# A 31-tap convolution on VectorE: three half-length filters with taps placed by hand, in a two-layer encoder

## The chip, the core and the metric

The kernel runs on one core of one Trainium2 chip. The metric is the device time of one execution in microseconds: 2544.08 us, the median of 3 runs (2543.35 to 2545.97). The engines are named as in the profile: PE (TensorE, matrix products), PEld (its weight loads), DVE (VectorE), ACT (ScalarE), POOL (GpSimd), SP (SyncE, which issues most DMAs).

## The reference

Input x is 1 x 1024 x 1024 (tokens by width) in float32; there are two layers. Each has a mixing part of three head groups, fed by one projection, and a feed-forward part.

```
for l in range(2):
    z = rms_norm(x, norm_mix[l]) @ w_in[l]        # 1024 -> 2560, 20 tiles of 128 columns
    (q_a, k_a, v_a, q_h, i_h, f_fw, f_bw, g_h, a_c, g_c) = split(z)
    o_att = attention(rope(rms_norm(q_a)), rope(rms_norm(k_a)), v_a)   # 8 heads, 2 for keys
    o_hg  = hgrn2_bidirectional(q_h, i_h, f_fw, f_bw, g_h)             # gated recurrence, both ways
    o_cv  = conformer_conv(a_c, g_c)
    x = x + concat[o_att, o_hg, o_cv] @ w_out[l]
    x = x + square(relu(rms_norm(x) @ w1[l])) @ w2[l]

def conformer_conv(a, gate, w_dw, b_dw, ln_g, ln_b):
    u = a * sigmoid(gate)                 # 256 channels x 1024 tokens
    y = depthwise convolution of u with w_dw, 31 taps, padded by 15 on both sides
    y = layer_norm(y + b_dw, ln_g, ln_b)  # over the channels
    return silu(y)
```

With taps w[-15] to w[15], the convolution of one channel is y[t] = sum over d of w[d] u[t + d], tokens outside 0 to 1023 being zero.

## The kernel before

Activations lie with channels on the 128 partitions and the 1024 tokens along the row, so a projection tile is 128 x 1024 float32: two banks of PSUM. A layer starts with 20 such tiles (`ztile`, `zsteps`), each 48 matmuls of 128x512 (L223: 8 slices of the input, three passes with high and low parts, two halves). DVE evacuates a tile by multiplying it with the norm's factors (L322, `evac`); two buffers of PSUM (S) serve the tiles in turn, so PE can be one tile ahead of DVE. For each tile DVE also makes the low part of the next weights (L200, wlo).

The order of a layer's first part in the program: tiles 16 and 18, 17 and 19 (`conv_in(0)`, `conv_in(1)`: two blocks of 128 channels), each pair giving u = a * sigmoid(s), by ACT and by POOL (L337). Then `Hgrn(0)`, half of the recurrence, takes tiles 6, 10, 12, 14, 8: from them come X (four arrays of 1024 tokens), T (decays), hks, the gate and iv, and iv is transposed on PE (L442) in the constructor. `core()` then runs it: `near()` (neighbouring tokens, L453 to L473), seven levels s = 1, 2, 4 to 64 of a doubling scheme, each with two multiplications of X on POOL and two on DVE (L525) and one of T (L526), and from s = 2 on with copies on ACT (L482), scores on PE (L494) and a masked write of them (L501, L505, predicated copies). Behind the levels stand Tc (L531, a copy of the decays), the transposes of the keys (L539), the chain of states (L555, L558) and the output (L583 on PE, L587 on DVE). Between these steps the loop at L702 asks two generators in turn, twice each: `qg`, the attention's projections (tile 5 for values, 4 for keys, 0 to 3 for queries, with statistics in `rstd`, L151 to L156, a rotation L621 to L624 and, for keys, L660), and `cg`, the convolution.

`conv(i)` is 31 DVE instructions on a row of 1024 for one block of channels: a first tap at d = 0 (L344, with the bias), then 30 taps (L352), each adding a shifted u times one weight to y in place:

```
nc.vector.scalar_tensor_tensor(
    y[:, lo:hi], u[:, lo + d : hi + d], par[:, l, wof + tap : wof + tap + 1], y[:, lo:hi],
    op0=ALU.mult, op1=ALU.add,
)
yield
```

After both blocks `conv_tail` takes the layer norm: token sums on PE (L162 in `tok_sums`), `rstd`, a widening copy on ACT (L168 in `widen`), a turn by PE (L178 in `flip`), and the subtraction or multiplication on DVE; the second half of it does the same for the squares.

Behind the loop `while not ys[1:]` (L706) finishes the second block. Then come `Hgrn(1)`, the recurrence's other half, with tiles 7, 11, 13, 15, 9 (its core is spread over the attention stage), the first two score units of the attention (`att_scores`) between its tiles 15 and 9, and the attention itself: 64 units. The projection w_out and the feed-forward part follow; the change touches nothing there.

The program's order is not the engines' order. The scheduler of the tile framework places each instruction on its engine by its place in the program and by its own estimates of when its inputs are there, so a tap that is asked for late in the program may come to stand earlier on DVE, between instructions that would wait. Buffers come from pools (x8: 8 rows of 128 x 1024, tmp: 4; small tiles nwa and nwt: 2 each), and a tile whose buffer is still in use waits for it.

## Time and profile before

| | |
|---|---|
| median of 3 runs | 2544.08 us (2543.35 to 2545.97) |
| profiled execution, its own time | 2543.87 us |
| its span, first to last instruction | 2541.9 us |
| PE busy | 2457.1 us (97%) |
| DVE busy | 1995.0 us (78%) |
| ACT busy | 1205.0 us (47%) |
| POOL busy | 736.7 us (29%) |

The profile is one execution seen by the hardware's profiler. Busy time is a sum over the span; an engine's share says little about a single stage, so the rows further down are cut into stages: from 58.66 us (the evacuation of the last tile of `conv_in`) over 117.61 (the evacuation of iv, behind the last tile of `Hgrn(0)`) and 221.17 (the states' chain) to 263.03 (the first evacuation of `Hgrn(1)`), 304.30 and 559.59 (most of the attention). The second layer's same points are 1321.70, 1380.60, 1483.80, 1525.60, 1566.90 and 1819.00. The time of the profiled execution and not the span is what compares with the median.

### The profile page before, as it was taken

To read this page: it belongs to the slowest core of one execution; us is meant where nothing else is said; L and a number is where in the kernel's file an instruction comes from. 1 tells how busy PE (TensorE), PEld (TensorE's weight loads), DVE (VectorE), ACT (ScalarE), POOL (GpSimd) and SP (SyncE) were. 2 spreads that over 40 slices of the span, in tenths; PEclk is the share of its full clock that TensorE was granted. 3 is DMA by queue.
4 is the path that set the end of the run, shared out by engine and by line. 5 is a ranking of instruction groups with operands and counts; after the bars stand their busy time and mean duration, and the time that the engine had idled before them with its cause. 6 is when DMAs were issued, how large, how long until landed. Compare 5 with 4: busy or idle time off the path is not lost.

```text
span 2541.9 us, 34037 instructions
## 1 busy us (share of the span) xinstructions
PE 2457.1 (97%) x12608; PEld 2023.4 (80%) x12608; DVE 1995.0 (78%) x3051; ACT 1205.0 (47%) x1960; POOL 736.7 (29%) x463
## 2 busy tenths in 40 slices
PE   8989989999999999999999899999999999999999
PEld 7777778878788887888887777788787888878887
DVE  5998598872887778987859985898628777789876
ACT  4222478773544444443433224787635444444332
POOL 0232565433034430000123324665330354300000
PEclk9999999999999999999999999999999999999999
DMA  4101210033244448454131113000322544584542
GB/s 149 68 25 63 95 43 18 14 106 115 75 165 164 144 158 322 159 174 156 67 108 50 42 63 104 17 18 26 124 84 91 178 141 154 185 287 158 162 153 91
DMA packets 113078, 286.99 MB, mean 113 GB/s; under 512 B 11409, under 2 KB 11665, under 8 KB 112913
## 3 DMA queue, kind: packets, MB, share of 16 engines
q1 hardware_dynamic: 112912, 284.83, 32.4%
q8 instruction: 99, 1.62, 0.3%
q14 instruction: 67, 0.54, 0.1%
HBM read 197.75 MB, written 87.03 MB: 112 GB/s over the span
## 4 chain that ended last, share of the span: by engine, by line
PE 78%; DVE 15%; ACT 3%; issue 2%; POOL 2%; DMA 0%; SPq 0%; DVEq 0%; ACTq 0%; POOLq 0%
PE S L223 15%; PE S L1196 10%; PE c L995 10%; PE S L995 7%; PE e L995 7%; PE e L1196 6%; PE c L1196 6%; DVE x L352 4%; PE e L803 4%; PE c L782 3%; PE S L745 3%; PE e L494 2%; DVE P L756 1%; PE e L162 1%; PE e L583 1%
## 5 line engine op out<-in xcount | busy, mean ns | idle before, releaser
L223 PE MATMUL S<-xs,whi 128*128 128x512 f32 x1280 | 366.3, 407 | 10.6 <-ACT xs L208 9.1
L223 PEld LDWEIGHTS S<-xs,whi 128*128 128x128 f32 x1280 | 245.0, 195 | 67.5 <-ACT xs L208 9.1
L1196 PE MATMUL S<-xs,xs 128*128 128x512 f32 x816 | 201.6, 390 | 2.6 <-DVE xs L897 2.6
L223 PE MATMUL S<-xs,wlo 128*128 128x512 f32 x640 | 204.0, 399 | 0.0
L896 ACT ACTIVATE xs<-m 128x512 fp32r<-128x512 f32 x216 | 126.0, 619 | 141.6 <-DVE m L907 50.8
L761 POOL TENSOR_SCALAR P<-P,mx 128x1024 f32<-128x1024 f32 x124 | 142.6, 1150 | 164.1 <-DVE mx L760 126.2
L787 DVE TENSOR_TENSOR PT<-c,PT 128x512 fp32r<-128x512 f32 x256 | 171.1, 684 | 24.2 <-ACT PT L786 22.6
L1196 PEld LDWEIGHTS S<-xs,xs 128*128 128x128 f32 x816 | 152.8, 188 | 35.5 <-DVE xs L897 3.5
L786 ACT ACTIVATE PT<-c 128x512 fp32r<-128x512 f32 x256 | 147.5, 593 | 69.1 <-PE c L782 65.5
L199 ACT ACTIVATE whi<-raw 128x1024 fp32r<-128x1024 f32 x56 | 59.1, 1058 | 247.1 <-PE S L223 234.1
L803 PE MATMUL e<-PT,x 128*128 128x256 f32 x1024 | 172.3, 297 | 0.8 <-ACT PT L786 0.5
L756 DVE TENSOR_SCALAR_CACHE_REDUCE P<-S,nqc 128x1024 f32<-128x1024 f32 x124 | 158.5, 1278 | 14.0 <-PE S L745 8.8
L352 DVE SCALAR_TENSOR_TENSOR x<-x,par,x 128x1009 f32<-128x1009 f32 (+14 forms) x120 | 166.8, 1390 | 1.8
L782 PE MATMUL c<-cons,P 128*128 128x128 f32 x992 | 152.4, 278 | 10.5 <-POOL P L761 5.6
L897 DVE TENSOR_TENSOR xs<-m,xs 128x512 fp32r<-128x512 f32 x216 | 144.9, 694 | 22.0 <-ACT xs L896 22.0
L745 PE MATMUL S<-x,QS 128*128 128x512 f32 x480 | 154.0, 419 | 4.8 <-DVE P L756 4.5
L260 POOL TENSOR_TENSOR tmp<-tmp,tmp 128x1024 f32<-128x1024 f32 x19 | 50.6, 2662 | 360.4 <-ACT tmp L259 360.2
L759 ACT ACTIVATE P<-P,mx 128x1024 f32<-128x1024 f32 x124 | 142.4, 1149 | 24.3 <-DVE P L756 23.0
L803 PEld LDWEIGHTS e<-PT,x 128*128 128x128 f32 x1024 | 139.0, 193 | 8.5 <-ACT PT L786 2.0
L223 PEld LDWEIGHTS S<-xs,wlo 128*128 128x128 f32 x640 | 123.2, 193 | 27.1 <-issue 0.3
L782 PEld LDWEIGHTS c<-cons,P 128*128 128x128 f32 x992 | 115.3, 141 | 36.7 <-issue 10.6
L1196 PE MATMUL e<-xs,xs 128*128 128x512 f32 x552 | 140.6, 390 | 0.3 <-DVE xs L897 0.3
(310 smaller groups left out, 5639.1 us busy)
## 6 DMA issues: line engine op xcount, KB each, us to landing
m<-ad SPq DMA_DIRECT2D x104, 512.0 KB, 3.8
ad<-x SPq DMA_DIRECT2D x176, 256.0 KB, 2.2
raw<-w_in_t SPq DMA_DIRECT2D x40, 512.0 KB, 3.4
xs<-w_t SPq DMA_DIRECT2D x36, 512.0 KB, 3.7
raw<-w_t SPq DMA_DIRECT2D x36, 512.0 KB, 3.7
m<-w_t SPq DMA_DIRECT2D x32, 512.0 KB, 6.8
ad<-tmp SPq DMA_DIRECT2D x48, 256.0 KB, 2.2
x<-w_t SPq DMA_DIRECT2D x24, 512.0 KB, 4.6
```

The costliest lines, as they stand in the source:

```text
L223: nc.tensor.matmul(zp[h] if type(zp) is list else zp[:, h, :], w, xx[:, h * 512 : (h + 1) * 512], start=first, stop=last)
L352: nc.vector.scalar_tensor_tensor(y[:, lo:hi], u[:, lo + d : hi + d], par[:, l, wof + tap : wof + tap + 1], y[:, lo:hi], op0=ALU.mult, op1= ...
L745: nc.tensor.matmul(S[:, hb, :], qs, kk[:, hb * 512 : (hb + 1) * 512], start=first, stop=not first)
L756: nc.vector.tensor_scalar(Pt, S, nqc[:, j, ci : ci + 1], 3.0e38, op0=ALU.mult, op1=ALU.min, accum_out=mx[:, 1:2])
L761: nc.gpsimd.tensor_scalar(Pt, Pt, mx[:, 3:4], 0.0, op0=ALU.mult, op1=ALU.add)
L782: nc.tensor.transpose(t[:, q * P : (q + 1) * P], Pt[:, hb, q * P : (q + 1) * P], ident)
L786: nc.scalar.activation(hi, src, AF.Copy)
L787: nc.vector.tensor_tensor(lo, src, hi.bitcast(F32), op=ALU.subtract)
L803: nc.tensor.matmul(pvp[:, cs], VS[g][:, hb * 4 + kb, :], pt[:, kb, :], start=hb == 0 and n == 0, stop=hb == 1 and n == 7,)
L897: ordered("v", nc.vector.tensor_tensor(lo, src, hi.bitcast(F32), op=ALU.subtract))
L995: nc.tensor.matmul(bank, w[i][:, kt * P : (kt + 1) * P], BC[name][kt][j], start=n == 0 and name not in ("M6", "M7", "M3"), stop=n == 11, s ...
L1196: nc.tensor.matmul(banks[dt], w[i][:, dt * P : (dt + 1) * P], a[j], start=n == 0 and name not in ("M6", "M7", "M3"), stop=n == 3 * SG - 1, ...
```

## The change

The convolution is computed in another way, and its instructions get other places.

Another way: the tokens are split into even ones ue and odd ones uo, 512 each. POOL writes u in this order (first all even tokens, then all odd ones). With s[n] = uo[n-1] + ue[n], the even taps as one filter E, the odd taps as one filter O and the sums of neighbouring taps as a third, a block of channels takes three filters of half the length: 15 taps on ue, 16 on uo and 16 on s. The even outputs are E(ue) + O(uo); the odd outputs are the third filter's result less the other two, with a correction at the row's end (`edge`). The third filter is written in place of uo. The bias comes in with the last combination, which writes y with every second token.

Other places: `taps(n)` asks the convolution's generator for n steps (two pieces each) at fixed points of the constructor of `Hgrn(0)` (6, 6, 6, 6, 5) and of `Hgrn(1)` (3, 4, 4, 4); in the loop of the core it is asked once in every second step after the fourth. A piece is also held behind the last instruction on the list `mark` (a level's predicated copy or the multiplication of T) by an order-only dependency. The transposes of iv move from the constructor to `turned()`, called in `near()` after its first step. The statistics of the keys are taken up at step 6 instead of 2 of the next tile, and `while not ys[1:]` is gone.

```diff
-            nc.gpsimd.tensor_tensor(u, a, s, op=ALU.mult)
+            nc.gpsimd.tensor_tensor(
+                u.rearrange("p (h n) -> p n h", h=2), a.rearrange("p (n h) -> p n h", h=2),
+                s.rearrange("p (n h) -> p n h", h=2), op=ALU.mult,
+            )
             us.append(u)
+        mark = []
+        def after_gate(i):
+            if mark:
+                tc.add_manual_dep(i.ins, mark[-1].ins.name, mybir.DependencyInfo(
+                    mybir.DependencyClass.NoSync, mybir.DependencyReason.DATA), reason="order")
+        def fir(dst, src, taps, shift=0):
+            n, m = dst.shape[1], src.shape[1]
+            for k, (d, w) in enumerate(sorted(taps, key=lambda t: abs(t[0] + shift))):
+                d += shift
+                lo, hi = max(0, -d), min(n, m - d)
+                if k == 0:
+                    nc.vector.tensor_scalar(dst, src[:, d : d + n], w, 0.0, op0=ALU.mult, op1=ALU.add)
+                else:
+                    after_gate(nc.vector.scalar_tensor_tensor(
+                        dst[:, lo:hi], src[:, lo + d : hi + d], w, dst[:, lo:hi], op0=ALU.mult, op1=ALU.add
+                    ))
+                yield
+        def conv_steps(i):
+            H = 512
+            ue, uo = halves(us[i])
+            both, mix = x8(), x8()
+            even, odd = halves(both)
...
+            hs = cst.t([P, 16], "nwa", bufs=2)
+            edge = cst.t([P, 16], "nwt", bufs=2)
...
+            s = mix[:, 0 : H + 1]
...
+            nc.vector.tensor_tensor(s[:, 1:H], uo[:, 0 : H - 1], ue[:, 1:H], op=ALU.add)
+            yield
+            second = fir(even, ue, [(d, tap(2 * d)) for d in range(-7, 8)])
+            for _ in fir(odd, uo, [(d, tap(2 * d + 1)) for d in range(-8, 8)]):
+                yield
+                if next(second, 1) is None:
+                    yield
+            yield from fir(uo, s, [(d, hs[:, d + 8 : d + 9]) for d in range(-8, 8)], 1)
+            y = mix.rearrange("p (n h) -> p n h", h=2)
+            cb = pv(l, "cb", i)
+            nc.vector.scalar_tensor_tensor(y[:, :, 0], even, cb, odd, op0=ALU.add, op1=ALU.add)
+            yield
+            nc.vector.tensor_tensor(uo[:, 0 : H - 1], uo[:, 0 : H - 1], even[:, 1:H], op=ALU.subtract)
+            nc.vector.tensor_tensor(uo[:, H - 1 : H], uo[:, H - 1 : H], edge[:, 8:9], op=ALU.subtract)
+            yield
+            nc.vector.scalar_tensor_tensor(y[:, :, 1], uo, cb, odd, op0=ALU.add, op1=ALU.subtract)
+            ys.append(mix)
+            yield
+
         def conv(i):
-            u = us[i]
-            y = x8()
...
+            for k, _ in enumerate(conv_steps(i)):
+                if k % 2:
+                    yield
+        def taps(n):
+            for _ in range(n):
+                next(cg, None)
...
                 evac(ztile(6 + ls), hq)
+                taps(3 if ls else 6)
...
-                    if ls == 1:
-                        next(cg, None)
...
+                    taps(4 if ls else 6)
...
+                if ls == 0:
+                    taps(5)
+
+            def turned(self):
                 for h in range(2):
                     tpv = pse()
...
                 yield
+                self.turned()
...
-                    if k == 2 and rest:
+                    if rest and k == (6 if col == 4 else 2):
...
-        for _ in h0.core():
-            for g in (qg, cg, qg, cg):
-                next(g, None)
+        for n, _ in enumerate(h0.core()):
+            next(qg, None)
+            if n > 3 and n % 2:
+                taps(1)
+            next(qg, None)
         drain(qg)
-        while not ys[1:]:
-            next(cg)
+        mark.clear()
```

What stands on the engines is shown at three places (a row is line, operation, written tile, read tiles, shape, count; lines are those of each kernel's own file).

DVE of the first layer, ahead of the evacuation of iv (the L322 that writes an m tile). Before, whole taps of block 0 stand between the evacuations of tiles 14 (tmp) and 8 (m); x_135 is its y, x_79 its u:

```order
L322 TENSOR_TENSOR tmp_651<-S_116_658,Rb_307 128x1024
L200 TENSOR_TENSOR wlo_717<-raw_714,whi_716 128x1024
L352 SCALAR_TENSOR_TENSOR x_135_807<-x_79_341,par_76,x_135_807 128x1017
L352 SCALAR_TENSOR_TENSOR x_135_807<-x_79_341,par_76,x_135_807 128x1016
L352 SCALAR_TENSOR_TENSOR x_135_807<-x_79_341,par_76,x_135_807 128x1015
L352 SCALAR_TENSOR_TENSOR x_135_807<-x_79_341,par_76,x_135_807 128x1014
L352 SCALAR_TENSOR_TENSOR x_135_807<-x_79_341,par_76,x_135_807 128x1013
L352 SCALAR_TENSOR_TENSOR x_135_807<-x_79_341,par_76,x_135_807 128x1012
L322 TENSOR_TENSOR m_118_713<-S_122_720,Rb_307 128x1024
```

With the change, these rows lead up to the same evacuation of iv; they are the end of block 0's third filter (x_79 is now the odd half that is written over, x_102 the tile of s and y) and its four combinations (L396, L393, L395 and L398 of the new file):

```order
L200 TENSOR_TENSOR wlo_775<-raw_772,whi_774 128x1024
L358 SCALAR_TENSOR_TENSOR x_79_341<-x_102_526,nwa_527,x_79_341 128x508
L358 SCALAR_TENSOR_TENSOR x_79_341<-x_102_526,nwa_527,x_79_341 128x506
L358 SCALAR_TENSOR_TENSOR x_79_341<-x_102_526,nwa_527,x_79_341 128x507
L358 SCALAR_TENSOR_TENSOR x_79_341<-x_102_526,nwa_527,x_79_341 128x505
L358 SCALAR_TENSOR_TENSOR x_79_341<-x_102_526,nwa_527,x_79_341 128x506
L396 TENSOR_TENSOR x_79_341<-x_79_341,nwt_528 128x1
L358 SCALAR_TENSOR_TENSOR x_79_341<-x_102_526,nwa_527,x_79_341 128x505
L393 SCALAR_TENSOR_TENSOR x_102_526<-x_101_525,par_76 128x512
L395 TENSOR_TENSOR x_79_341<-x_79_341,x_101_525 128x511
L398 SCALAR_TENSOR_TENSOR x_102_526<-x_79_341,par_76,x_101_525 128x512
L322 TENSOR_TENSOR m_122_771<-S_126_778,Rb_307 128x1024
```

Six taps of 1012 to 1017 tokens stood there; now pieces of some 506 tokens stand there, and block 0 is finished before iv is evacuated.

DVE behind Tc, in the statistics of the queries (nwa, nwt, nwy: `rstd`). Before, x_200 is block 1's y, m_227 the states:

```order
L154 SCALAR_TENSOR_TENSOR nwt_1563<-nwy_1562 128x16
L558 SCALAR_TENSOR_TENSOR m_227_1493<-m_227_1493,Tc_1490,e_1583 128x64
L155 TENSOR_TENSOR nwt_1563<-nwt_1563,nwa_1561 128x16
L352 SCALAR_TENSOR_TENSOR x_200_1289<-x_91_460,par_76,x_200_1289 128x1018
L156 SCALAR_TENSOR_TENSOR nwy_1562<-nwt_1563,nwy_1562 128x16
L558 SCALAR_TENSOR_TENSOR m_227_1493<-m_227_1493,Tc_1490,e_1583 128x64
L154 SCALAR_TENSOR_TENSOR nwt_1563<-nwy_1562 128x16
L352 SCALAR_TENSOR_TENSOR x_200_1289<-x_91_460,par_76,x_200_1289 128x1017
L155 TENSOR_TENSOR nwt_1563<-nwt_1563,nwa_1561 128x16
L558 SCALAR_TENSOR_TENSOR m_227_1493<-m_227_1493,Tc_1490,e_1583 128x64
L156 SCALAR_TENSOR_TENSOR nwy_1562<-nwt_1563,nwy_1562 128x16
L555 COPY m_227_1493<-e_1621 128x64
```

With the change, behind its Tc, the statistics of a query tile alternate with pieces of block 1's first filters (x_127 holds even and odd, x_91 is u):

```order
L156 SCALAR_TENSOR_TENSOR nwy_1469<-nwt_1470,nwy_1469 128x16
L358 SCALAR_TENSOR_TENSOR x_127_832<-x_91_460,par_76,x_127_832 128x506
L154 SCALAR_TENSOR_TENSOR nwt_1470<-nwy_1469 128x16
L358 SCALAR_TENSOR_TENSOR x_127_832<-x_91_460,par_76,x_127_832 128x506
L155 TENSOR_TENSOR nwt_1470<-nwt_1470,nwa_1468 128x16
L358 SCALAR_TENSOR_TENSOR x_127_832<-x_91_460,par_76,x_127_832 128x506
L156 SCALAR_TENSOR_TENSOR nwy_1469<-nwt_1470,nwy_1469 128x16
L358 SCALAR_TENSOR_TENSOR x_127_832<-x_91_460,par_76,x_127_832 128x505
L154 SCALAR_TENSOR_TENSOR nwt_1470<-nwy_1469 128x16
L358 SCALAR_TENSOR_TENSOR x_127_832<-x_91_460,par_76,x_127_832 128x505
L155 TENSOR_TENSOR nwt_1470<-nwt_1470,nwa_1468 128x16
L358 SCALAR_TENSOR_TENSOR x_127_832<-x_91_460,par_76,x_127_832 128x505
```

Two taps of block 1 stood among twelve rows; now six pieces do, each between two dependent small instructions.

PE of the first layer, at the second turn of `conv_tail` (L162 the token sums of the squares, L178 the turn of the widened factors). Before:

```order
L162 MATMUL e_2026<-cons_77,tmp_1959 128x1 x8
L223 MATMUL S_310_2089<-xs_103,whi_1878 128x512 x2
L223 MATMUL S_310_2089<-xs_104,whi_1878 128x512 x2
L223 MATMUL S_310_2089<-xs_103,wlo_1879 128x512 x2
L223 MATMUL S_310_2089<-xs_115,whi_1878 128x512 x2
L223 MATMUL S_310_2089<-xs_116,whi_1878 128x512 x2
L223 MATMUL S_310_2089<-xs_115,wlo_1879 128x512 x2
L223 MATMUL S_310_2089<-xs_120,whi_1878 128x512 x2
L223 MATMUL S_310_2089<-xs_121,whi_1878 128x512 x2
L223 MATMUL S_310_2089<-xs_120,wlo_1879 128x512 x2
L223 MATMUL S_310_2089<-xs_125,whi_1878 128x512
L178 MATMUL e_2051<-cons_77,tmp_2049 128x128 x4
```

With the change (L802 are the first scores of the attention, S_319 and S_322):

```order
L802 MATMUL S_319_2206<-x_274_1849,x_272_1841 128x512 x2
L162 MATMUL e_2150<-cons_77,tmp_2086 128x1 x8
L802 MATMUL S_319_2206<-x_275_1850,x_272_1841 128x512 x2
L802 MATMUL S_322_2217<-x_274_1849,x_272_1841 128x512 x2
L802 MATMUL S_322_2217<-x_275_1850,x_272_1841 128x512 x2
L178 MATMUL e_2175<-cons_77,tmp_2173 128x128 x4
L178 MATMUL e_2182<-cons_77,tmp_2173 128x128 x4
```

Before, 19 projection matmuls stood between the sums and the turn; now 6 score matmuls do.

## Rows read from the trace of the kernel before

**Rows 1.** The page: busy time of the engines; the chain by engine and line.
```profile
PE 2457.1 (97%) x12608; PEld 2023.4 (80%) x12608; DVE 1995.0 (78%) x3051; ACT 1205.0 (47%) x1960; POOL 736.7 (29%) x463
...
PE 78%; DVE 15%; ACT 3%; issue 2%; POOL 2%; DMA 0%; SPq 0%; DVEq 0%; ACTq 0%; POOLq 0%
PE S L223 15%; PE S L1196 10%; PE c L995 10%; PE S L995 7%; PE e L995 7%; PE e L1196 6%; PE c L1196 6%; DVE x L352 4%; PE e L803 4%; PE c L782 3%; PE S L745 3%; PE e L494 2%; DVE P L756 1%; PE e L162 1%; PE e L583 1%
```

**Rows 2.** Windows by stage: window, length, busy us, clock, DMA.
```profile
core 0: us, PE busy (x) PEld busy (x) DVE busy (x) ACT busy (x) POOL busy (x), PEclk, DMA share, GB/s
58.66:117.61 58.95, 55.95 (x247) 45.98 (x245) 56.87 (x43) 16.48 (x16) 11.37 (x4) 1.00 0.20 72
117.61:221.17 103.56, 91.80 (x519) 72.75 (x519) 99.87 (x136) 29.22 (x43) 40.42 (x19) 0.90 0.13 44
221.17:263.03 41.86, 40.93 (x309) 32.60 (x310) 34.87 (x68) 8.28 (x10) 11.54 (x3) 0.96 0.18 64
...
1380.60:1483.80 103.20, 92.06 (x519) 73.02 (x519) 96.79 (x135) 29.26 (x43) 40.07 (x19) 0.90 0.13 44
...
304.30:559.59 255.29, 243.90 (x1689) 205.58 (x1690) 213.51 (x406) 194.80 (x338) 148.15 (x115) 0.99 0.14 45
1566.90:1819.00 252.10, 240.36 (x1660) 202.06 (x1661) 210.77 (x403) 192.02 (x334) 148.55 (x115) 0.99 0.13 41
```

**Rows 3.** The chain of waits, 60 to 330 us: by line; start, us, what.
```profile
by line: PE S L223 26.9%; DVE x L352 17.7%; issue 8.5%; DVE wlo L200 4.9%; PE e L162 4.5%; DVE X L525 3.8%; DVE A L505 3.4%; DVE tmp L322 2.7%; PE e L583 2.7%; DVE T L526 2.3%; DVE nwt L154 2.0%; DVE nwt L155 1.7%; DVE tmp L623 1.6%; DVE tm
...
58.85 10.67 PE S L223 x47
```

**Rows 4.** Waits, 58.66 to 263.03 us: us in total, times, longest us.
```profile
DVE ms L678 <- PE e L162: 7.0, 4, 2.9
...
PE e L637 <- DVE A L501: 4.2, 1, 4.2
```

**Rows 5.** Lines of DVE, 58.66 to 263.03 us: busy us, mean ns, idle before.
```profile
L352 DVE SCALAR_TENSOR_TENSOR x<-x,par,x 128x1009 f32<-128x1009 f32 (+14 forms) x60 | 83.5, 1392 | 0.9
...
L344 DVE TENSOR_SCALAR x<-x,par 128x1024 f32<-128x1024 f32 x2 | 3.7, 1844 | 0.0
```

**Rows 6.** Timeline of DVE: start us, us, instruction and count.
```profile
71.81 9.14 DVE L352 SCALAR_TENSOR_TENSOR x<-x,par,x 128x1012 f32<-128x1012 f32 x7
...
118.74 1.28 DVE L453 TENSOR_TENSOR m<-X 128x512 f32<-128x512 f32 x2
119.94 2.53 DVE L200 TENSOR_TENSOR wlo<-raw,whi 128x1024 fp32r<-128x1024 f32 x1
...
179.89 0.17 DVE L156 SCALAR_TENSOR_TENSOR nwy<-nwt,nwy 128x16 f32<-128x16 f32 x1
180.01 1.28 DVE L352 SCALAR_TENSOR_TENSOR x<-x,par,x 128x1022 f32<-128x1022 f32 x1
181.21 0.01 DVE L621 LOAD_MASK_SELECT tmp<-tmp  x1
```

**Rows 7.** Lines of DVE, whole span: ns min/median/max; a form, mean ns.
```profile
L344 DVE TENSOR_SCALAR x<-x,par x4: 804/806/2882, 61.4 to 1411.9; 128x1024 f32<-128x1024 f32 x4
...
L1008 DVE SCALAR_TENSOR_TENSOR x<-x,Rb 128x512 f32<-128x512 f32 x64 | 42.5, 684 | 0.1
```

**Rows 8.** DVE and POOL: two timelines, one line, one group.
```profile
98.99 5.93 DVE L352 SCALAR_TENSOR_TENSOR x<-x,par,x 128x1020 f32<-128x1020 f32 x3
...
99.15 3.38 POOL L449 TENSOR_TENSOR m<-m,m 128x1024 f32<-128x1024 f32 x1 [35.41 <-DVE m L423]
...
L337 POOL TENSOR_TENSOR x<-tmp,tmp x4: 2394/2508/2877, 44.2 to 1324.1; 128x1024 f32<-128x1024 f32 x4
...
L525 POOL TENSOR_TENSOR X<-X,T 128x512 f32<-128x512 f32 x14 | 24.5, 1769 | 37.0 <-ACT m L482 25.3 <-DVE m L453 6.8 <-DVE T L526 4.9
```

**Rows 9.** Waits of PE, whole span: us in total, times, longest us.
```profile
PE e L442 <- DVE m L322: 11.4, 4, 4.3
PE e L178 <- ACT tmp L168: 7.9, 4, 2.8
```

More of the change, by code (lines that the diff above doesn't have):

```diff
@@ L336, in conv_in @@
             u = x8()
-            nc.gpsimd.tensor_tensor(u, a, s, op=ALU.mult)
+            nc.gpsimd.tensor_tensor(
+                u.rearrange("p (h n) -> p n h", h=2), a.rearrange("p (n h) -> p n h", h=2),
+                s.rearrange("p (n h) -> p n h", h=2), op=ALU.mult,
+            )
             us.append(u)
-        def conv(i):
-            u = us[i]
-            y = x8()
-            wof = PAR["cw"][0] + i * CK
-            nc.vector.tensor_scalar(
-                y, u, par[:, l, wof + CPAD : wof + CPAD + 1], pv(l, "cb", i), op0=ALU.mult, op1=ALU.add
-            )
-            for tap in range(CK):
-                d = tap - CPAD
-                if d == 0:
-                    continue
-                lo, hi = max(0, -d), min(L, L - d)
-                nc.vector.scalar_tensor_tensor(
-                    y[:, lo:hi], u[:, lo + d : hi + d], par[:, l, wof + tap : wof + tap + 1], y[:, lo:hi],
-                    op0=ALU.mult, op1=ALU.add,
-                )
-                yield
-            ys.append(y)
+        mark = []
@@ new lines, in conv_steps @@
+        def conv_steps(i):
[3 more added lines that the diff above has]
+            even, odd = halves(both)
+            wof = PAR["cw"][0] + i * CK
+            tap = lambda d: par[:, l, wof + d + CPAD : wof + d + CPAD + 1]
+            hs = cst.t([P, 16], "nwa", bufs=2)
+            edge = cst.t([P, 16], "nwt", bufs=2)
+            nc.vector.tensor_copy(hs[:, 0:1], tap(-CPAD))
+            nc.vector.tensor_tensor(
+                hs[:, 1:16], par[:, l, wof + 1 : wof + CK - 1 : 2], par[:, l, wof + 2 : wof + CK : 2], op=ALU.add
+            )
+            nc.vector.tensor_tensor(
+                edge[:, 0:7], ue[:, H - 7 : H], par[:, l, wof + 1 : wof + CPAD : 2], op=ALU.mult
+            )
+            nc.scalar.activation(edge[:, 0:7], edge[:, 0:7], AF.Copy, accum_out=edge[:, 8:9])
+            s = mix[:, 0 : H + 1]
+            nc.scalar.activation(s[:, 0:1], ue[:, 0:1], AF.Copy)
+            nc.scalar.activation(s[:, H : H + 1], uo[:, H - 1 : H], AF.Copy)
+            nc.vector.tensor_tensor(s[:, 1:H], uo[:, 0 : H - 1], ue[:, 1:H], op=ALU.add)
[16 more added lines that the diff above has]
+            yield
@@ L425, in __init__ @@
                 evac(ztile(14 + ls), gl)
-                if ls == 1:
-                    next(cg, None)
+                taps(4 if ls else 6)
                 gate = tmp()
@@ L441, in __init__ @@
                         c = h * 4 + q
-                        nc.tensor.transpose(tpv[:, q * P : (q + 1) * P], iv[:, c * P : (c + 1) * P], ident)
+                        nc.tensor.transpose(tpv[:, q * P : (q + 1) * P], self.iv[:, c * P : (c + 1) * P], ident)
                     nc.scalar.activation(
-                        vt[:, h * 4 : h * 4 + 4, :], tpv.rearrange("p (a b) -> p a b", a=4), AF.Copy
+                        self.vt[:, h * 4 : h * 4 + 4, :], tpv.rearrange("p (a b) -> p a b", a=4), AF.Copy
                     )
@@ L504, in scores @@
                         else:
-                            nc.vector.copy_predicated(
+                            mark.append(nc.vector.copy_predicated(
                                 dst, masks[:, lev].unsqueeze(1).to_broadcast([P, 4, P]), src
-                            )
+                            ))
                     yield
@@ L525, in core @@
                         eng.tensor_tensor(xv, xv, tv, op=ALU.mult)
-                    nc.vector.tensor_tensor(
+                    mark.append(nc.vector.tensor_tensor(
                         Tv[:, :, :, 0, 0], Tv[:, :, :, 0, 0], Tv[:, :, :, 1, 0], op=ALU.mult
-                    )
+                    ))
                     yield
@@ L768, in tile_hybrid_trunk @@
         drain(cg)
+        mark.clear()
         xsp.close()
```

## The prediction

> **What bounds the kernel now.** I read the page first, then the windows by stage, the chain, the waits of two engines, and last single instructions. The page has TensorE (PE) busy for 97% of the span, and PE lines make up 78% of the chain; yet 15% of it is VectorE (DVE), and L352, the convolution tap, is the DVE line with most of it [rows 1]. So the reader should look for the one stage where DVE sets the pace. The windows show it: from 117.61 to 221.17 us DVE is busy for 99.87 of 103.56 us, PE for 91.80, at a granted clock of 0.90; from 58.66 to 117.61 DVE has 56.87 of 58.95. After 221.17 the balance turns: PE 40.93 of 41.86, DVE 34.87 [rows 2]. The second layer repeats it: 103.20 us for the middle stretch, DVE 96.79. The chain through 60 to 330 us says the same, with L352 second behind the projections at 17.7% [rows 3]. What PE waits for there is DVE: 4.3 us for the evacuation L322 ahead of the transposes L442 [rows 9], and 4.2 us where the value transposes (L637) stand behind DVE work [rows 4]. Outside this stage (one in each layer) the change touches nothing but the order of the attention stage.
>
> **The taps.** In the stretch 58.66 to 263.03 us all of one layer's convolution runs on DVE: 60 taps, 83.5 us busy, and two first taps, 3.7 us [rows 5]. Seven taps in a row, each reading what the last one wrote, take 9.14 us, 1.31 us each; a tap with an independent instruction behind it gives way after 1.20 us (180.01 to 181.21) [rows 6]. In the order of before 24 taps follow directly on the tap they read: 24 x 1.31 + 36 x 1.20 + 2 x 0.80 = 76.2 us. Against durations (60 x 1.28, an undisturbed tap in [rows 6], + 1.6 = 78.4) the busy time of 87.2 holds another 9 us: taps that stood still while POOL worked, as the three that took 5.93 us beside POOL's multiplication at 99.15 [rows 8].
>
> Now each of two convolutions has 47 half-length pieces (15 even, 16 odd, 16 on sums): 3 TENSOR_SCALAR and 44 SCALAR_TENSOR_TENSOR of 504 to 512 elements, 4 additions and combinations of the same length, 4 tiny ones. The form exists before: L1008, 684 ns, at 128x512 [rows 7]. From start to start two independent 512-element instructions take 1.20 us (118.74 to 119.94) [rows 6], 0.60 each; a dependent one I put at 0.684 plus the small gap of the long chain, 0.71. Even and odd pieces alternate, so only about 9 of 88 in a layer follow directly on what they read: 79 x 0.60 + 9 x 0.71 = 53.8. Six TENSOR_SCALAR at half of 0.804 [rows 7] are 2.4, eight additions and combinations 4.8, eight tiny ones 0.09 each (a tiny one's start to the next, 179.89 to 180.01, is 0.12 at most [rows 6]) 0.7. Sum 61.7 us: 14.5 less than 76.2, per layer. Bounds: with all pieces at 0.71, TENSOR_SCALAR at the full 0.80 and tiny ones at 0.17 it is 62.5 + 4.8 + 5.7 + 1.4 = 74.4, 1.8 saved; below 0.60 nothing in the rows goes. I take the low cost, because the alternation stands in the order and the 0.60 is measured for just that case. The POOL stalls I leave at 9 us: POOL has the same instructions.
>
> The pair that gave 0.60 overlaps. The Trainium skill (VectorE: DVE Perf Modes, The DRAIN you can't avoid) says that the next DVE instruction does not start until the pipeline is empty; by that every piece would cost its full duration, the saving would be the 1.8 of the upper bound, and the time 2544. This trace disagrees for independent neighbours (0.60 against 0.68) and agrees for dependent ones.
>
> The four combinations per layer write every second element. L453 reads and writes every second element too, and is that same pair at 0.60 [rows 6], so I add nothing. The Trainium skill (Vector Engine (DVE) Microarchitecture Reference, 5.2 Measured stream behaviour on trn2) wants runs of two adjacent words and puts a hopping destination at 1.71 ns an element instead of 1.05: an estimate of 4 x 0.34 = 1.4 us per layer, the time then 2522. No row here shows it.
>
> The first multiplication L337 now writes in two halves. POOL takes 2.5 us for it [rows 8]; were it twice as long, its result for the first convolution (started at 44.2 us) would still be there before DVE comes to taps at 61, and the second is wanted only some 25 us after it ends: nothing. The three tiny copies per convolution on ScalarE cost nothing either: it is busy for 16.48 of 58.95 us there [rows 2].
>
> **The places.** From tile 19's evacuation to the state decay copy (Tc, L531) the order of before has 123 instructions that are not conv, the order now 103: 20 fewer (predicated copies, rotary steps, small statistics). They come back behind Tc, and so does conv: 24 pieces between Tc and the first output addition L587 where there were 9 taps, and 8 more ahead of the second recurrence's first evacuation (263.03), where there were 3. So the middle stretch should shrink by about 20 us and the stretch behind it grow by about 6: DVE had 7 us to spare there (41.86 less 34.87, [rows 2]). The sum over both is what counts, the 14.5.
>
> Three smaller terms. The key statistics (11 tiny dependent instructions) lose the taps between them: 11 x 0.11 = +1.2 us. Conv's second statistics now stand with 6 score matmuls ahead of the flip L178 instead of 19 projection matmuls; cover falls from 19 x 0.227 = 4.3 us (47 of them take 10.67, [rows 3]) to 6 x 0.227 = 1.4, and L178 waits already now, 7.9 us in four [rows 9]: I take +2.2, bounds 0 and +2.9. The value transposes of the second half-layer move behind the first attention work: L442 waits 11.4 us in four, of which the first and its twin are 4.3 each and go with the DVE time; the other two, 1.4 each, go by the move: -1.4. The attention stage itself is re-ordered; its two copies, 255.29 and 252.10 us, differ by 3 us with the same work [rows 2], and so much I allow either way.
>
> Per layer -14.5 + 1.2 + 2.2 - 1.4 = -12.5, twice -25.0. The profiled execution took 2543.87 us (span 2541.9), 0.2 below the median shown: 2518.9, so **2519 us**.
>
> **Rivals.**
> (a) *More: DVE's own waits go too.* DVE waits 7.0 us for q statistics in the stage [rows 4], and PE's slower clock, 0.90, comes behind its waits. If the spread of taps fills these, -20 per layer: 2504. For: PE has slack there (91.80 of 103.56 with slow stretches). Against: they are waits for PE, which will be busier.
> (b) *Nothing.* Levels of the recurrence form a loop: ScalarE copies, PE scores, DVE predicated copies, POOL multiplications. POOL's 14 multiplications are 24.5 us and wait 25.3 for ScalarE's copies [rows 8]. If that loop yields only half of the freed time (some 7 us), the longer tail takes it back: 2544. Pieces at their upper cost end here as well. Against: ScalarE is busy for 29.22 and POOL for 40.42 of 103.56 us [rows 2], DVE for nearly all.
> (c) *Slower.* The loop sets the middle stretch alone and it keeps its 103.6 us. Then the DVE work now behind Tc lengthens the last stretch by 7 us in full, and the two waits added come on top: 7 + 1.2 + 2.2 - 1.4 = 9 per layer, 2562. It decides from the point where the middle stretch gives less than 9 us.
>
> **How the numbers follow.** Forecast 0.61 (its own range 2508 to 2532, from the 0.60/0.71 choice, L178 and 3 us of attention), (a) 0.18, (b) 0.12, (c) 0.09. 0.2% of this time, 5 us, is what a measurement can tell from no change. Faster: 0.61 + 0.18 + 0.03 of (b)'s edge = 0.82; same 0.09; slower 0.09. The range 2500 to 2541 takes in the forecast, most of (a), and stops short of (b).
>
> **What would show it.** Right: 94 pieces per layer at 0.68 to 0.70 us median; the middle stretch under 90 us with the clock above 0.90; the stretch behind Tc longer, DVE over 95% busy in it; the 4.3 and 4.2 us waits of PE smaller; everything from the feed-forward on as before. Wrong: pieces near 0.8 us or more; the middle stretch over 95 us; a new PE wait at L178 or at the first scores above 4 us in each layer.

## The result, and the profile after

The changed kernel takes 2552.64 us (median of 6, 2549.71 to 2555.92), the kernel before 2543.61 us (median of 6); the ratio is 1.0035, with a 95% interval of 1.0025 to 1.0046. It is slower by about 9 us, where 2519 was forecast. The profiled execution took 2555.92 us, the longest of the six, so the windows below hold some 3 us more than the median. One execution, of 4929.81 us, of the kernel listed further down as "... and without moves" is left out of its ratio.

The page of the profiled execution after (busy time; the chain by engine and by line):

```profile
PE 2461.8 (96%) x12608; PEld 2022.0 (79%) x12608; DVE 1976.2 (77%) x3147; ACT 1204.7 (47%) x1976; POOL 711.2 (28%) x463
...
PE 75%; DVE 9%; ACT 2%; POOL 2%; issue 2%; DMA 1%; SPq 0%; DVEq 0%; POOLq 0%; ACTq 0%
PE S L223 13%; PE S L1254 10%; PE c L1053 10%; PE S L1053 7%; PE e L1053 7%; PE e L1254 7%; PE c L1254 6%; PE c L840 3%; PE e L861 3%; PE S L802 3%; PE e L550 2%; DVE x L358 2%; PE e L639 1%; DVE P L813 1%; PE e L162 1%
```

Read against [rows 1] this is what the change was to do: DVE's share of the chain went from 15% to 9%, its busy time from 1995 to 1976 us. It is no time won, because a chain's shares say who was last, not what the next one would have cost. The windows say where the time went. The stages of the first layer after (window, length, busy us of PE, PEld, DVE, ACT and POOL, clock), and the second layer's middle stretch:

```profile
core 0: us, PE busy (x) PEld busy (x) DVE busy (x) ACT busy (x) POOL busy (x), PEclk, DMA share, GB/s
57.47:118.23 60.76, 57.08 (x252) 46.96 (x250) 60.55 (x76) 17.25 (x22) 9.86 (x4) 1.00 0.20 69
118.23:199.31 81.08, 74.28 (x410) 57.25 (x411) 70.43 (x104) 24.61 (x39) 33.71 (x18) 0.92 0.11 40
199.31:258.78 59.47, 57.17 (x405) 45.82 (x404) 50.07 (x121) 11.56 (x15) 10.85 (x4) 0.94 0.20 67
258.78:322.53 63.75, 56.12 (x268) 46.09 (x266) 26.56 (x43) 27.38 (x30) 24.83 (x14) 0.95 0.26 87
322.53:583.70 261.17, 247.42 (x1712) 206.39 (x1713) 220.76 (x409) 196.04 (x340) 135.14 (x109) 0.99 0.14 47
1388.37:1466.07 77.70, 71.21 (x410) 55.32 (x411) 70.39 (x105) 24.63 (x39) 33.58 (x18) 0.96 0.12 41
```

Against [rows 2]: the middle stretch fell from 103.56 to 81.08 us, as forecast and more. But from Tc to the first evacuation of `Hgrn(1)` it grew from 41.86 to 59.47. The matmul records show why: the middle stretch held 519 of them before and 410 now, the next one 309 before and 405 now. Tc came earlier, PE's projections did not. Over the whole stage, 57.47 to 258.78, it is 201.31 us where 204.37 were, 3.1 less; PE is busy for 188.5 in both. The two stretches that follow had been, before (no rows of these stand above):

```profile
263.03:318.80 55.77, 52.00 (x256) 42.51 (x254) 29.39 (x54) 27.51 (x30) 27.70 (x14) 1.00 0.29 96
318.80:576.70 257.90, 246.51 (x1714) 207.80 (x1715) 217.87 (x408) 195.50 (x338) 136.69 (x109) 0.99 0.15 49
```

So `Hgrn(1)`'s tiles take 63.75 us instead of 55.77 (+8.0), and the attention stage 261.17 instead of 257.90 (+3.3). The second layer has the same pattern (stage 203.96 to 197.35, tiles 55.0 to 63.8; from there to w_out's last addition 323.8 to 326.1).

Much of the 8.0 us is seen on PE behind the second token sums (start, us, instruction; in brackets the idle time ahead and its releaser):

```profile
296.87 1.95 PE L162 MATMUL e<-cons,tmp 128*128 128x1 f32 x16 [1.33 <-POOL tmp L433]
298.67 1.63 PE L802 MATMUL S<-x,x 128*128 128x512 f32 x6
302.24 1.09 PE L178 MATMUL e<-cons,tmp 128*128 128x128 f32 x8 [1.93 <-ACT tmp L168]
306.83 2.04 PE L223 MATMUL S<-xs,whi 128*128 128x512 f32 x4 [3.50 <-DVE x L813]
```

L162, the sums of the squares, waits 1.33 us for POOL; six score matmuls (L802) follow; the turn L178 waits 1.93; and then tile 9 waits 3.50 for DVE's L813, the first softmax, which holds the buffer that tile 9 needs and stands on DVE behind the layer norm's last multiplications (303.00 to 305.48). PE resumes at the low clock (granted 0.50, the level of 1.2 GHz, from 306.83 to 308.90): the first four matmuls take 2.04 us where later groups of four take 1.07. Before, the layer norm was done by then, and between the scores and tile 9 PE waited for 0.41 us in all. But the kernel before has a wait in the same stretch that the changed one has not, at the first turn:

```profile
269.30 1.09 PE L178 MATMUL e<-cons,tmp 128*128 128x128 f32 x8 [2.77 <-ACT tmp L168]
```

So the three waits, 6.8 us, are 3.6 more than the 3.2 of before. The low clock adds some 2 us (ten matmuls from 306.83 to 311.07 take 4.2 us, where ten take 2.3 [rows 3]); the rest of the 8.0 was not taken apart.

PE's waits over the whole span (us, times, longest), with [rows 9]:

```profile
PE e L497 <- DVE m L322: 9.4, 2, 4.9
...
PE S L223 <- DVE x L813: 7.0, 2, 3.5
...
PE e L178 <- ACT tmp L168: 4.3, 4, 1.9
```

The wait for iv's evacuation (L442 before, L497 now) fell from 11.4 in four to 9.4 in two: the moved transposes wait no longer, but the first and its twin wait 4.9 and 4.5, where they were 4.3 at most and should have shrunk with DVE's work. L178 fell too, from 7.9 to 4.3: the term I had feared is smaller, and its neighbour, 7.0 us at L223, is new.

### The profile page after: what moved, and what is told of

Read it like the earlier page. It is cut to its first block, busy times and chain, and to the rows that moved or that the text cites. A ratio compares the mean times of both kernels' runs of the same rounds, so it can differ in the third digit from the quotient of the medians.

```text
span 2552.3 us, 34175 instructions
## 1 busy us (share of the span) xinstructions
PE 2461.8 (96%) x12608; PEld 2022.0 (79%) x12608; DVE 1976.2 (77%) x3147; ACT 1204.7 (47%) x1976; POOL 711.2 (28%) x463
## 4 chain that ended last, share of the span: by engine, by line
PE 75%; DVE 9%; ACT 2%; POOL 2%; issue 2%; DMA 1%; SPq 0%; DVEq 0%; POOLq 0%; ACTq 0%
PE S L223 13%; PE S L1254 10%; PE c L1053 10%; PE S L1053 7%; PE e L1053 7%; PE e L1254 7%; PE c L1254 6%; PE c L840 3%; PE e L861 3%; PE S L802 3%; PE e L550 2%; DVE x L358 2%; PE e L639 1%; DVE P L813 1%; PE e L162 1%
## 5 line engine op out<-in xcount | busy, mean ns | idle before, releaser
L223 PE MATMUL S<-xs,whi 128*128 128x512 f32 x1280 | 367.8, 409 | 16.2 <-ACT xs L208 7.7
L223 PEld LDWEIGHTS S<-xs,whi 128*128 128x128 f32 x1280 | 244.9, 195 | 73.5 <-issue 10.1
L223 PE MATMUL S<-xs,wlo 128*128 128x512 f32 x640 | 204.2, 400 | 0.0
L813 DVE TENSOR_SCALAR_CACHE_REDUCE P<-S,nqc 128x1024 f32<-128x1024 f32 x124 | 158.6, 1279 | 14.1 <-PE S L802 9.2
L199 ACT ACTIVATE whi<-raw 128x1024 fp32r<-128x1024 f32 x56 | 59.1, 1057 | 217.0 <-PE S L223 196.4
L802 PE MATMUL S<-x,QS 128*128 128x512 f32 x480 | 153.7, 423 | 6.2 <-DVE P L813 6.0
L223 PEld LDWEIGHTS S<-xs,wlo 128*128 128x128 f32 x640 | 123.7, 194 | 27.0 <-issue 0.2
L1254 PE MATMUL c<-xs,xs 128*128 128x512 f32 x552 | 139.2, 390 | 0.0
```

The costliest lines, as they stand in the source:

```text
L223: nc.tensor.matmul(zp[h] if type(zp) is list else zp[:, h, :], w, xx[:, h * 512 : (h + 1) * 512], start=first, stop=last)
L802: nc.tensor.matmul(S[:, hb, :], qs, kk[:, hb * 512 : (hb + 1) * 512], start=first, stop=not first)
L813: nc.vector.tensor_scalar(Pt, S, nqc[:, j, ci : ci + 1], 3.0e38, op0=ALU.mult, op1=ALU.min, accum_out=mx[:, 1:2])
L1254: nc.tensor.matmul(banks[dt], w[i][:, dt * P : (dt + 1) * P], a[j], start=n == 0 and name not in ("M6", "M7", "M3"), stop=n == 3 * SG - 1, ...
```

## Experiments

All ratios are to the kernel before on the same chip. "Stage" is from conv_in's last evacuation to the first of `Hgrn(1)`, "tiles" from there to the evacuation of its iv; both are given for layer 1. With the key statistics moved, the first evacuation of `Hgrn(1)` stands earlier among the work, so that only the sum of the two compares (253.6; before 260.1, filters alone 251.1).

| kernel | median us | ratio (95%) | stage | tiles |
|---|---|---|---|---|
| before | 2543.61 | 1 | 204.4 | 55.8 |
| the change | 2552.64 | 1.0035 (1.0025 to 1.0046) | 201.3 | 63.8 |
| filters alone | 2528.16 | 0.9934 (0.9918 to 0.9951) | 194.4 | 56.6 |
| places alone | 2573.53 | 1.0112 (1.0097 to 1.0127) | 207.4 | 65.7 |
| few taps | 2512.26 | 0.9867 (0.9852 to 0.9882) | 189.6 | 52.9 |
| layer norm put back | 2545.90 | 1.0007 (0.9998 to 1.0016) | 197.0 | 60.7 |
| filters + table + gates | 2543.78 | 1.0003 (0.9994 to 1.0013) | 199.7 | 59.1 |
| filters + table | 2549.88 | 1.0033 (1.0019 to 1.0047) | 202.9 | 56.8 |
| filters + transposes moved | 2532.27 | 0.9959 (0.9943 to 0.9975) | 195.2 | 56.6 |
| filters + key statistics moved | 2534.82 | 0.9973 (0.9961 to 0.9984) | 183.1 | 70.5 |
| fewer early steps | 2541.36 | 0.9996 (0.9987 to 1.0005) | 191.6 | 66.4 |
| store put back | 2545.77 | 1.0012 (1.0001 to 1.0024) | 197.0 | 58.7 |
| fewer steps, store put back | 2541.41 | 0.9988 (0.9978 to 0.9998) | 189.0 | 64.7 |
| ... and without moves | 2541.35 | 0.9984 (0.9975 to 0.9994) | 190.2 | 63.1 |
| early layer norm | 2545.94 | 1.0015 (1.0006 to 1.0024) | 198.6 | 62.8 |
| gates alone | 2584.31 | 1.0165 (1.0150 to 1.0180) | 204.6 | 73.8 |

**Filters alone.** The kernel before with `conv_steps` and the de-interleaved write, in the old loop:

```diff
         for _ in h0.core():
             for g in (qg, cg, qg, cg):
-                next(g, None)
+                if g is qg or not ys[1:]:
+                    next(g, None)
```

> The kernel before with the half-length filters and the de-interleaved write, and nothing else: no gates, no new places, transposes and key statistics as before. Theory T (PE was idle for only 15.7 us of the 204 in the stage, so less DVE work can give little): 3 to 6 us less per layer than before, 2532 to 2538. Rival P (the saving of DVE comes through in full and the places ate it): 10 to 12 per layer, 2520 to 2524. Rival N (the filters give nothing): 2544.

2528.16 us. Layer 1 in windows, the four stretches and the whole stage:

```profile
57.69:116.00 58.31, 55.95 (x247) 45.99 (x245) 56.51 (x66) 16.64 (x18) 9.79 (x4) 1.00 0.21 72
116.00:213.60 97.60, 90.91 (x520) 71.61 (x521) 93.13 (x156) 29.62 (x47) 34.62 (x19) 0.93 0.13 44
213.60:252.13 38.53, 37.85 (x288) 29.51 (x287) 30.81 (x63) 7.15 (x10) 9.64 (x3) 0.96 0.14 48
252.13:308.76 56.63, 56.20 (x274) 46.19 (x273) 27.97 (x60) 27.57 (x30) 26.58 (x13) 0.97 0.33 107
57.69:252.13 194.44, 184.71 (x1053) 147.10 (x1052) 180.45 (x282) 53.41 (x74) 54.04 (x26) 0.96 0.16 53
```

The stage lost 9.9 us (204.37 to 194.44), nearly all that DVE lost (191.61 to 180.45); `Hgrn(1)`'s tiles stay within 1 us of before. In the old order the filters give two thirds of the forecast, 0.66% or some 17 of 25 us; the theory that PE leaves them little was too low, its rival P too high.

**Few taps.** The kernel before with `if abs(d) > 3: yield; continue` among the taps (the outer 24 taps of each block left out).

> The kernel before with 7 taps a block instead of 31 (the convolution's outer 24 taps are left out): some 63 us less DVE work in each layer's stage, a bound on what any faster convolution can give. Theory T (PE sets the stage): at most PE's 15.7 idle us per layer and part of its slow stretches, 8 to 16 per layer, 2512 to 2528. Rival P (DVE sets it, as I predicted): 25 or more per layer, below 2495.

2512.26. The stage:

```profile
57.55:247.10 189.55, 182.69 (x1073) 146.22 (x1072) 127.02 (x212) 54.08 (x70) 56.27 (x27) 0.97 0.18 62
```

With DVE at 127.02 us instead of 191.61, the stage is still 189.55 long, and PE busy for 182.69 of it. Theory T held, at its lower end. For this order it bounds what any faster convolution can give: of 64.6 us less DVE work, 14.8 come through. The first 11 us of DVE work that the filters save bring 9.9, the next 53 bring 4.9.

**Places alone.** The changed kernel with full-length taps in its places:

```diff
-            for k, _ in enumerate(conv_steps(i)):   # three half-length filters
-                if k % 2:
+            for k, _ in enumerate(conv_steps(i)):   # 30 full-length taps
+                if k % 5 < 4:
                     yield
```

> The changed kernel with its places, gates and moves, but the full-length taps of before in 24 steps a block (every fifth step holds two). Theory T: the layer norm comes as late as in the changed kernel or later and DVE has its old work, so it is slower than before by 5 to 9 us per layer: 2554 to 2562. Rival R (places cost nothing by themselves): 2543 to 2547.

2573.53, 11 us above the upper end. The two longest waits of PE:

```profile
PE e L514 <- DVE x L662: 13.0, 2, 6.9
PE e L461 <- DVE m L322: 11.9, 2, 6.3
```

The scores' matmuls (L514) wait behind value work on DVE, a wait that the kernel before has not. The transposes (L461) wait for iv's evacuation, 6.3 us at most, where the kernel before has 4.3 at most [rows 9]; that it is taps which hold the evacuation up is a reading of the order. With -0.66% for the filters and +1.12% for the places, the sum, +0.46%, is near the change's +0.35%, and within the intervals: taken whole, the two about add up.

**Layer norm put back.** In the changed kernel:

```diff
-                taps(3 if ls else 6)
+                if ls == 0:
+                    taps(6)
...
-                taps(4 if ls else 6)
+                taps(1 if ls else 6)
...
+        while not ys[1:]:
+            next(cg)
         mark.clear()
```

> The changed kernel with the three steps of the convolution's layer norm asked for where they were before: the second block finished ahead of Hgrn(1), then one step after its tiles 11, 13 and 15. Theory T (the changed kernel lost its gain because the second statistics now stand among the first scores: PE waits 1.3, 1.9 and 3.5 us there in each layer and starts tile 9 at the low clock): these three waits go, the stretch from the first evacuation of Hgrn(1) to the last falls from 63.8 to about 56 us, and the whole kernel by 14 to 18, to 2535 to 2539 us. Rival R (what is lost is lost in the attention stage, by its new order): 2549 to 2553.

2545.90, a ratio of 1.0007: 6.7 us less, half of the forecast; the tiles fell to 60.7 us, where about 56 were expected. The first scores now have this one wait on PE, where 1.33, 1.93 and 3.50 stood:

```profile
298.77 1.21 PE L805 MATMUL S<-x,x 128*128 128x512 f32 x4 [0.41 <-DVE tmp L322]
```

Of the three waits only tile 9's 3.50 is gone. The other two moved to between the tiles, 1.3 us at L162 and 1.1 at L178, so that PE waits 2.8 us in the stretch where it waited 6.8. Theory T had the right place and half the size; the late layer norm is not all of the loss.

**The table and the gates.** The changed kernel with its layer norm put back, first without the two moves (transposes in the constructor, key statistics at step 2), then also with `if False:` for `if mark:`.

> The changed kernel with the layer norm's steps of before, and with the two moves undone: what is left beside the filters is the table of taps and the gates. Theory G: 2541 to 2546, as high as with the moves (2545.9). Rival M: 2528 to 2533.

> As the run before it, without the order-only dependencies on the recurrence: the table of taps alone. If the gates cost it, 2528 to 2533; if the table does (block 1's pieces asked for earlier or later than the scheduler would take them), as with gates, 2541 to 2546.

2543.78, as theory G has it, and 2549.88, above both forecasts: the table of taps costs, and the gates, which I suspected, win some of it back (the two intervals lie just apart). PE's waits in the stage, first of the filters alone, then of the table, then of table and gates:

```profile
PE e L490 <- DVE m L322: 3.6, 1, 3.6
...
PE e L685 <- DVE A L549: 1.1, 1, 1.1
```

```profile
PE e L499 <- DVE m L322: 7.0, 1, 7.0
PE e L694 <- DVE A L558: 5.5, 1, 5.5
```

```profile
PE e L499 <- DVE m L322: 6.1, 1, 6.1
...
PE e L694 <- DVE A L558: 3.4, 1, 3.4
...
PE e L551 <- DVE tmp L717: 2.3, 1, 2.3
```

The wait for iv's evacuation is 3.6, 7.0 and 6.1 us, that of the value transposes 1.1, 5.5 and 3.4; PE is idle in the stage for 9.7, 15.8 and 15.1 us in all. The order suggests why: of 110 convolution instructions (tiny ones included), 55 stand ahead of iv's evacuation with the filters alone, 69 with the table, 66 with the table and the gates; ahead of the evacuation of tile 6 it is 11, 19 and 19. In these orders a piece that the program asks for between two tiles stands on DVE ahead of the next evacuation, while of those that it asks for later the scheduler took fewer that early. That this costs the time is argued from the order and the waits; the run with fewer early steps, below, bears it out only in part.

**The two moves.** `turned()`, and `k == (6 if col == 4 else 2)`, each added to the filters alone:

> The half-length filters in the order of before, plus one move of the change: the transposes of iv behind the first step of near(). The filters alone took 2528.2. Theory G (of the 17.7 us that the changed kernel with its layer norm put back has over the filters alone, the gates and the table of taps cost nearly all): 2527 to 2530. Rival M (the moves cost it): 2533 to 2538 here or in the run on the keys.

> The half-length filters in the order of before, plus the key statistics taken up at step 6 instead of 2. Theory G: 2527 to 2530. Rival M: 2533 to 2538.

2532.27, between the two forecasts, and 2534.82, as rival M has it: the ratios are higher by 0.25% and 0.39%, the first within both intervals' reach, the second not. Beside table and gates the two together add 0.04% (1.0003 to 1.0007), so they are not what made the change slower.

**Fewer early steps.** `taps(4)` for `taps(6)` in `Hgrn(0)`, on the kernel with the layer norm put back:

> The changed kernel with the layer norm's steps of before and with 4 steps of the convolution instead of 6 at the four places between the tiles of Hgrn(0) (without it 2545.9, ratio 1.0007). Theory T (58 half-length pieces asked for in the constructor stand ahead of the evacuations: DVE is full there, the evacuation of iv comes late and PE waits 4.9 us for it in each layer): that wait falls below 2 us and the kernel to 2534 to 2540, ratio 0.996 to 0.9985. Rival R (where in the stage the pieces stand does not matter, the recurrence behind it does): 2544 to 2549, the wait moving elsewhere.

45 instructions stand ahead of iv's evacuation, its wait on PE is gone, and the stage fell from 197.0 to 191.6 us, as theory T has it. But the time, 2541.36, lies between the two forecasts: the ratio fell by only 0.11%, under 3 us, where the stages of the two layers lost 11.3. The stage and the tiles behind it:

```profile
56.65:248.21 191.56, 186.34 (x1074) 149.63 (x1073) 167.02 (x275) 54.04 (x75) 53.95 (x26) 0.96 0.17 60
248.21:314.59 66.38, 55.87 (x259) 45.16 (x257) 33.74 (x68) 26.45 (x29) 25.63 (x14) 0.93 0.27 84
```

DVE's work in the tiles is 33.74 us, where it was 25.55: block 1's last 14 instructions now stand behind the first evacuation of `Hgrn(1)`, and the layer norm is late again. The loss moved on, as the rival said.

**The gate's store.** On SP in the changed kernel, near 315 us, the store of the gate (L485) stands between the two loads of the second keys (L770, L771); ACT's split (L205) and behind it DVE's and iv's evacuation wait for the second load:

```profile
312.68 0.45 SPq L770 DMA_DIRECT2D tmp<-kd  x1
...
315.76 0.33 SPq L485 DMA_DIRECT2D gd<-tmp  x1
316.13 0.45 SPq L771 DMA_DIRECT2D tmp<-kd  x1
```

```profile
320.24 1.06 ACT L205 ACTIVATE x<-tmp 128x1024 fp32r<-128x1024 f32 x1 [7.00 <-DMA tmp<-kd]
```

With the store asked for in `near()` instead, SP has:

```profile
305.73 0.45 SPq L777 DMA_DIRECT2D tmp<-kd  x1
306.23 0.59 SPq L778 DMA_DIRECT2D tmp<-kd  x1
...
308.86 0.49 SPq L517 DMA_DIRECT2D gd<-tmp  x1
```

> The changed kernel with the layer norm's steps of before, and the gate's store of Hgrn(1) asked for later, so that on SP both loads of the second key half stand ahead of it again, as in the kernel before. Theory Q (SP waits at the store for POOL's gate, the second load and with it ACT's and DVE's key split and the evacuation of iv come 2.6 us late in each layer): the stretch from the first softmax to that evacuation falls from 16.0 to 13.5 us, the whole by 5, ratio 0.9985 to 0.999. Rival: it is hidden, 1.0007 as before.

The stretch from the first softmax to iv's evacuation fell from 16.0 to 14.1 us (14.5 in layer 2), but the time did not: 1.0012 beside 1.0007. In the profile of this kernel the stage of layer 2 is 200.3 us long, where it was 196.3, which takes back what the tiles of both layers gained. The wait is real, its cost for the whole is not shown.

**Both, and both without the moves.**

> The changed kernel with the layer norm's steps of before, 4 early steps instead of 6, and the gate's store behind the key loads on SP. Theory S (the two hide each other: what fewer early steps win in the stage is lost at the store): below both, 2531 to 2537, ratio 0.9955 to 0.9975. Rival A (the loss moves on into the attention stage): 2539 to 2543, as with fewer early steps alone.

> As the run before it, with the transposes of iv and the key statistics where they were before the change: what is left of the change are the filters, a smaller table and the gates. If the moves cost 1 to 4 us per layer also here: 2526 to 2533, ratio 0.9935 to 0.996, near the filters alone. If they are neutral: as the run before it.

2541.41 and 2541.35. Theory S fell and rival A held: nothing adds up below fewer steps alone by more than the intervals. Without the moves it is as with them. The stages, 189.0 and 190.2 us, are as short as with few taps, but the tiles still take 64.7 and 63.1 us.

**Early layer norm and gates alone.** Filters alone with `conv_tail` run in the loop too; and filters alone with the gates.

> The filters alone, with the convolution's layer norm also taken in the loop of the recurrence's first half instead of between the tiles of Hgrn(1). Theory T (where the layer norm meets projection matmuls on PE its waits are covered): as fast as the filters alone or up to 5 us faster, 2522 to 2529. Rival: its DVE work (5 us per layer) lands in the stage where PE waits for DVE, 2531 to 2538.

> The filters in the order of before with the gates alone: since the convolution is asked for only in the loop of the recurrence, its pieces cannot be taken up between the tiles of Hgrn(0), where DVE then idles, and the work stands behind. Theory: the constructor gets shorter by 4 us and the stage behind it longer by more: 2532 to 2542. Rival (DVE has room enough): 2526 to 2530.

2545.94, 8 us above the rival's upper end, and 2584.31. Early, the layer norm lengthens the stage by 4.1 and the tiles by 6.1 us; PE's waits in that kernel:

```profile
PE e L178 <- ACT tmp L168: 10.0, 6, 3.2
...
PE e L162 <- POOL tmp L416: 6.3, 2, 3.1
```

With the filters alone L178 waits 5.3 us in four. The gates alone hold block 0 back until the recurrence has begun: 15 instructions stand ahead of iv's evacuation, DVE has room there, and 78 crowd between it and Tc. PE then waits for the states (L631), for evacuations and for the value transposes:

```profile
PE e L631 <- DVE m L606: 15.3, 2, 9.2
PE S L223 <- DVE m L322: 13.2, 2, 6.6
PE e L685 <- DVE A L549: 10.7, 2, 5.4
```

The direction was foreseen; the size was not: 4 to 14 us over the filters alone were expected, 56 came.

## Why the prediction was wrong

**The step that failed is "The places".** It weighed the middle stretch and the one behind it by DVE alone: 20 us less there, 6 more here, because DVE had 7 us to spare. The first half held (22.5 less). The second was 17.6: Tc moved forward and PE's projections did not, so that some 100 matmuls changed stretch, and PE, busy for 40.93 of 41.86 us there [rows 2], had no room to take them up. DVE, by which the step weighed that stretch, ended up busy for 50.07 of 59.47 us in it, 84%, where the prediction wanted over 95%. So two of its signs of being right, the middle stretch under 90 us and the clock above 0.90, came true while the whole got slower. What the places cost, such as PE's longer waits for evacuations, had no term; the three small ones summed to +2 per layer. By ratios the steps from one kernel to the next are: filters -0.66%; table of taps +0.99%; gates -0.30%; the two moves +0.04%; late layer norm +0.28%; sum +0.35%. What I put at +2 per layer is +1.01% together, some 13 us per layer: per layer the filters give -8.4 where -14.5 stood, the places +12.9 where +2.0 stood, in all +4.5 where -12.5 stood. These are steps along one path and not prices that add in any order: on the filters alone the gates cost 2.3%, beside the table they win 0.30%. Which parts of the table cost its 0.99% is only argued.

**The taps.** The mechanism was right, the saving too large, because every cost was too low. A piece takes 743 ns, not 684. It starts 0.66 us after its neighbour, not 0.60, when it does not read what that one wrote, and 0.78 after it, not 0.71, when it does. DVE of the changed kernel (13 alternating pieces; five that follow on each other beside POOL; a combination; iv's evacuation):

```profile
73.29 8.64 DVE L358 SCALAR_TENSOR_TENSOR x<-x,par,x 128x509 f32<-128x509 f32 x13
...
108.60 6.75 DVE L358 SCALAR_TENSOR_TENSOR x<-x,nwa,x 128x508 f32<-128x508 f32 x5
...
116.17 0.75 DVE L393 SCALAR_TENSOR_TENSOR x<-x,par 128x512 f32<-128x512 f32 x1
...
118.23 1.22 DVE L322 TENSOR_TENSOR m<-S,Rb 128x1024 f32<-128x1024 f32 x1
```

Three pieces that follow on each other undisturbed, in the filters alone, have starts 0.78 us apart:

```profile
1348.98 2.31 DVE L358 SCALAR_TENSOR_TENSOR x<-x,nwa,x 128x512 f32<-128x512 f32 x3
```

In the changed kernel 7 of a layer's 88 stand directly behind the one that they read: 81 x 0.66 + 7 x 0.78 + 6 x 0.40 + 8 x 0.66 + 0.7 = 67.3 us, so 8.9 are saved and not 14.5; the filters alone shortened the stage by 9.9. The 0.60 was from L453, a tensor_tensor of two tiles, and the 684 ns from L1008, whose factor is the constant 0.0; a piece takes its factor from the parameters, and the line of the filters alone has a median of 741 ns:

```profile
L358 DVE SCALAR_TENSOR_TENSOR x<-x,par,x x116: 719/741/1600, 64.0 to 1465.1; 128x511 f32<-128x511 f32 x16, 128x510 f32<-128x510 f32 x16, 128x509 f32<-128x509 f32 x16, 128x508 f32<-128x508 f32 x16
```

The combinations, which write every second element, take 0.75 us like the pieces that write all. The prediction set against its overlap what the Trainium skill (VectorE: DVE Perf Modes, The DRAIN you can't avoid) says of an empty pipeline; the same paragraph there lets a next instruction that is not held start earlier, so the overlap was no disagreement. The price of a hopping destination that the Trainium skill (Vector Engine (DVE) Microarchitecture Reference, 5.2 Measured stream behaviour on trn2) led me to estimate, 1.4 us per layer, is not seen here; the row that I took it from is for hops of 4 KiB, where these are of 8 bytes. POOL's de-interleaved write takes as long as the plain one (L337: 2593 ns in the median of four, 2508 before).

**L178.** The cover I counted by matmuls was the wrong cost: L178 waits less than before. What came with the late layer norm was the softmax behind it on DVE, and through it the buffer of tile 9: 3.5 us in each layer, and the low clock behind it. I had named who waits for L178, not what stands behind the layer norm on DVE.

**The rivals.** (c) had the sign, and a wrong mechanism: the middle stretch did give, and more than the 9 us from which it was to decide. (b) is nearer in time, and had the tail take back what the middle stretch gave, but what took it was not the recurrence's loop, since the middle stretch, where that loop stands, gave 22.5 us. I had no rival in which the places themselves cost, though the order showed 66 half-length instructions ahead of iv's evacuation where 28 taps had stood.

**Open.** The stage of the kernel with fewer steps is shorter than that of the filters alone (191.6 and 194.4), its tiles longer by 9.8; a table that has the first without the second was not found. The 3.3 us in the attention stage were not taken apart, and there is more there: with the layer norm put back, stage and tiles of both layers are 6.1 us shorter than before, yet the profiled execution took 2544.10 us against 2543.87, so that some 6 us are lost behind the tiles. Each block holds one of the two buffers of nwa and of nwt for its whole length, which leaves the statistics one; whether the filters alone lose time by it is not tested, because with four of each the kernel does not fit in the core's memory (56 kb a partition were wanted, 55.78 were there). The fastest kernel that computes everything is the filters alone, 0.66% or some 17 us under the kernel before.

## What to carry to other kernels

Where two engines are both near full in a stage, bound a saving on one by a kernel with most of its work left out: here, in one stage, 65 us less of DVE's work were worth 15. Count, in the order of an engine, what fillers stand ahead of each evacuation that another engine needs, and time both sides: the 55 that the scheduler put there by itself were the fastest, 66 and 69 made PE wait longer, and 15, held back by the gates, crowded behind and cost most. A change with a better computation and a new order is two changes, and each is to be timed alone.

## What the runs showed of the hardware

A scalar_tensor_tensor of 512 elements with its factor in the parameters takes 741 ns, one with the factor 0.0 684 (L1008); a tap of 1024 elements 1280 [rows 6]. That the factor makes the difference is likely and not shown, since the two also read different tiles. Half the length is 0.58 of the time. A neighbour that does not read the result starts 0.66 us after it, 0.08 before its end; one that reads it starts 0.78 after it, 0.04 behind its end. Taps of 1024 tokens had the same pattern, 1.20 and 1.31.
